# A two-layer hybrid decoder trunk: products that nothing reads on TensorE in the mixer, and the second attention group's score products over 128 rows

## The chip, the cores and the metric

The kernel runs on one core of a Trainium2 chip. TensorE (PE) multiplies matrices, VectorE (DVE), ScalarE (ACT) and GpSimd (POOL) do the rest, and SyncE (SP) issues most DMAs; POOL issues some too. The metric is the device time of one execution in microseconds; of several runs the median counts.

## The reference, cut to what matters

Two layers on x of 512 tokens by 1024 channels in float32. Each layer is a half-step SwiGLU feed-forward, a token mixer with three groups of heads, and a second half-step feed-forward; a layer norm follows each.

```
x = layer_norm(ALPHA * x + 0.5 * swiglu(x, ffn_a_gate, ffn_a_up, ffn_a_down))
aq, ak, av, bq, bk, bv, cc = split(x @ w_in)
o_a = rms_norm(diff_attention(rope(aq), rope(ak), av, lam)) * (1 - lambda_init)
o_b = rms_norm(dilated_attention(rope(bq), rope(bk), bv))
o_c, v_first = rwkv7_mixer(cc, ...)
x = layer_norm(ALPHA * x + concat([o_a, o_b, o_c]) @ w_out)
x = layer_norm(ALPHA * x + 0.5 * swiglu(x, ffn_b_gate, ffn_b_up, ffn_b_down))
```

Group A is differential attention, group B dilated attention (here one causal score matrix with a bias from the counts of its three patterns), group C RWKV-7 time mixing.

## The kernel before, in words

Every float32 operand of a large product is split into a high part, rounded to float32r, and a low part, the rest. A product is then three: high by high, high by low, low by high. The activations stand transposed, channels on partitions, in two tiles for the whole kernel, `xhi` and `xlo`, of 128 by 8 by 512 (channel within a block, block, token). A token block of 128 is written into them by `channel_ops`: for each half of the channels four PE transposes into a PSUM tile `m`, ACT's copy of it into `xhi`, DVE's difference into `xlo`. x0 to x3 are the four token blocks; x2 and x3 come late (`LATE`).

Accumulators in PSUM have the tags `p0`, `p1`, `m` and `r`, two buffers each. In a trace `p0` and `p1` both read p.

The two feed-forwards of a layer are long rows of products on PE. Between them stands the mixer, class `Mix`, whose engines follow an order written out by hand. Its parts are generators, named in `RANK` (line 1444), that yield the names of what they need next. `Board.merge` picks the next part whose needs are met at the time that the model gives PE, else the one whose needs are met first. The model is in `Board`: `free` is the time at which each engine is free, `ready` holds for each tensor the end of its last write, by tensor and not by the piece written, `slots` the times at which buffers of a tag came free. `Board.note` places each instruction: it starts when its engine is free and all tensors that it names are ready. `Watched` (line 470) records every mixer instruction there and then issues it, which is why they all bear line 504 in the profile. A DMA is taken to land 2 us after its transfer. The times exist only while the program is built; they set the order, and the hardware waits for semaphores.

In time a mixer goes: x2 and x3 arrive (`arrive`) while `columns` makes the input projection by 256-column products; group A's units, then group B's, run with the RWKV parts between them; then `out` forms the output product from the mixed heads, which `mixer_tiles` (tiles o) and `mixer_tiles_c` (tiles yc) transpose into `xhi` and `xlo`, blocks 0 to 5 and 6 to 7; then the norm, the transposes of the new x0 to x3, and `head`, the first products of the second feed-forward.

The attention groups read q and k from HBM, where `turner` wrote them; `fetch` loads them by POOL's DMA queue. For group B a unit of 128 queries makes its scores by two products: q high and low (128 rows, 64 each) by k high twice, and q high (64 rows) by k low, tile `k2`, 64 rows.

Of the kernel before, what the change touches and what calls it, by code (L numbers as in the profile page):

```python
# [9 lines left out]
FR = mybir.dt.float32r  # L10
# [6 lines left out]
S = 512  # L17
# [10 lines left out]
class Trunk:  # L28
    def __init__(self, ctx, tc, consts):
        self.tc, self.nc = tc, tc.nc  # L30
        pool = lambda name, **kw: ctx.enter_context(tc.tile_pool(name=name, bufs=1, **kw))
        self.const = pool("const")
        self.psum = pool("psum", space=PSUM)
        self.consts = consts
        self.xhi = self.const.tile([128, KD, S], FR, name="xhi")
        self.xlo = self.const.tile([128, KD, S], FR, name="xlo")
        self.open_x()
        kept = self.const.tile([128, 130], FT, name="kept")
        self.nc.sync.dma_start(kept, consts[:, 0:130])
        self.ident, self.pick = kept[:, 0:128], kept[:, 128:130]  # L40
        self.warmed = False
# [321 lines left out]
class Board:  # L363
# [6 lines left out]
    def __init__(self, tc):  # L370
        self.tc = tc
        self.free = {}
        self.ready = {}
        self.slots = {}
        self.events = {}
        self.last = self.late = 0.0
        nc = tc.nc
        for name, engine in (("pe", nc.tensor), ("vec", nc.vector), ("act", nc.scalar), ("pool", nc.gpsimd), ("sp", nc.sync)):
            self.free[name] = 0.0
            setattr(self, name, Watched(self, name, engine))  # L380
        self.free["dma"] = 0.0
# [18 lines left out]
    def note(self, name, fn, aps, cost):  # L400
        at = self.free[name]
        tiles = [self.ready.setdefault(a.tensor.name, [0.0, "", 0.0, None]) for a in aps]
        assert all(r[3] != "dropped" for r in tiles)
        dma = fn == "dma_start"
        for r in tiles[dma and tiles[0][1] == "dma":]:
            if r[1] != name or name != "pe":
                at = max(at, r[0] + 0.134)
        end = at + cost
        self.free[name] = end
        if dma:  # L410
            n = 4
            for d in aps[0].shape:
                n *= d
            end = max(end, self.free["dma"]) + n / 340e3
            self.free["dma"] = end
            end += 2.0
        for r in tiles:
            r[2] = max(r[2], end)
        tiles[0][0] = max(tiles[0][0], end)
        tiles[0][1] = "dma" if dma else name  # L420
        if dma:
            self.late = max(self.late, end)
        elif name != "pe":
            self.last = max(self.last, end)

    def when(self, spec, tail):
        at = 0.0
        need = {}
        for s in spec:
            if s == ".":  # L430
                at = max(at, tail)
            elif isinstance(s, str):
                if s in self.slots or s in TAGS:
                    need[s] = need.get(s, 0) + 1
                elif s in self.events:
                    at = max(at, self.events[s])
                else:
                    return None
            else:
                at = max(at, self.ready[s.tensor.name][0])  # L440
        for tag, n in need.items():
            free = self.slots.get(tag)
            if free is not None:
                if len(free) < n:
                    return None
                at = max(at, sorted(free)[n - 1])
        return at

    def merge(self, streams):

# [63 lines left out]
class Mix:  # L514


    def __init__(self, tr, pool, above, p, l, dram, v_first, small):
# [22 lines left out]
        self.kr, self.bk, self.am, self.bt, self.yt, self.uv, self.gam, self.key = {}, {}, {}, {}, {}, {}, [], []  # L540
        self.kd = dram.tile([2, 2, 128, S], FT, name=f"kr{l}")

    def run(self):
        with self.tr.tc.manual_schedule(engines=MANUAL):
            self.board.merge([getattr(self, name)(*args) for name, *args in RANK])
        return self.ahead

    def arrive(self):

        tr = self.tr  # L550
        for t in range(NT):
            self.board.ready[tr.x[t].tensor.name] = [ARRIVE[t], "vec", ARRIVE[t], None]
        self.board.free["vec"] = ARRIVE[-1]
        self.board.free["pe"] = START
        for t in LATE:
            yield from tr.channel_ops(t, self.pe, self.act, self.vec, self.acc, self.drop)
            self.mark(f"x{t}")
        for t in range(NT):
            self.sp.dma_start(self.spill[t], tr.x[t])
# [202 lines left out]
    def fetch(self):  # L762

        dma = self.gps.dma_start
        ap = lambda t, off, dims: bass.AP(tensor=t.tensor, offset=t.offset + off, ap=dims)
        for grp in "AB":
            for hp in range(3):
                for e in range(2):
                    yield f"qk{grp}{hp}", "x", "x"
                    if (hp, e) == (0, 0):  # L770
                        yield f"qk{grp}{hp}", "x", "x", "bias"
                        self.bias = self.get("bias", "bias")
                        dma(self.bias, self.tr.consts[:, 130:642] if grp == "A" else self.tr.consts[:, 642:1154])
                    a = self.get("x", "q", (128, 2, S), FR)
                    d = self.qk[grp, hp]
                    hi, lo, k = e * 64 * S, (256 + e * 64) * S, 128 * S
                    if grp == "A":
                        b = self.get("x", "k", (128, 2, S), FR)
                        dma(a[0:64], ap(d, hi, [[256 * S, 2], [2 * S, 32], [1, 2 * S]]))
                        dma(b[0:64], ap(d, hi + k, [[0, 2], [2 * S, 32], [1, 2 * S]]))  # L780
                        dma(a[64:96], ap(d, hi, [[2 * S, 32], [1, 2 * S]]))
                        dma(b[64:96], ap(d, lo + k, [[2 * S, 32], [1, 2 * S]]))
                    else:
                        b = self.get("x", "k2", (64, S), FR)
                        dma(a[:, 0, :], ap(d, hi, [[256 * S, 2], [S, 64], [1, S]]))
                        dma(a[:, 1, :], ap(d, hi + k, [[0, 2], [S, 64], [1, S]]))
                        dma(b, ap(d, lo + k, [[S, 64], [1, S]]))
                    self.qkt[grp, hp, e] = a, b
                    self.mark(f"q{grp}{hp}{e}")

# [428 lines left out]
    def attend(self, grp):  # L1219
        tr, vec, act, pe = self.tr, self.vec, self.act, self.pe  # L1220
# [5 lines left out]
        def scores(x):  # L1226
            hp, e, qt = x["id"]
            n = (qt + 1) * 128
            nn = max(n, 256)
            qs = slice(qt * 128, (qt + 1) * 128)  # L1230
            x["l"] = self.t("l", (128, 2), bufs=8)
            x["p"] = []
            a, b = x["qk"]
            for m in range(M):
                sc = self.acc("p1")
                if isA:
                    pe.matmul(sc[:, :nn], a[0:96, m, qs], b[0:96, m, :nn], start=True, stop=True)
                else:
                    pe.matmul(sc[:, :nn], a[:, 0, qs], a[:, 1, :nn], start=True, stop=False)
                    pe.matmul(sc[:, :nn], a[0:64, 0, qs], b[:, :nn], start=False, stop=True)  # L1240
                t = self.get("t", "t")
                nm = self.t("nm", (128, 1), bufs=8)
                vec.tensor_tensor_reduce(t[:, :n], sc[:, :n], bias[:, S - n:], scale, 3e38, op0=OP.add, op1=OP.min,
                                         accum_out=nm)
                self.drop(sc)
                act.activation(t[:, :n], t[:, :n], AF.Exp, scale=-1.0, bias=nm, accum_out=x["l"][:, m:m + 1])
                x["p"].append(t)
# [32 lines left out]
        units = [{"id": (hp, e, qt)} for hp in range(3) for e in range(2) for qt in range(NT)]  # L1280
        L1, L2, L3 = LAGS[grp]
        n = len(units)
        for i in range(n + L3):
            if i < n:
                x = units[i]
# [17 lines left out]
            if L1 <= i < n + L1:  # L1303
                x = units[i - L1]
                yield x["p"][-1], 
                combine(x)
            if L2 <= i < n + L2:
                x = units[i - L2]
                yield x["p"][0], "m", "aT"
                turn(x)  # L1310
            if L3 <= i < n + L3:
                x = units[i - L3]
# [127 lines left out]
                        yield ()  # L1440


LAGS = {"A": (1, 2, 3), "B": (1, 3, 4)}
RANK = [("arrive",), ("decays",), ("weights",), ("keys", 0), ("keys", 1), ("inside",), ("invert", 0), ("attend", "A"), ("scan",), ("attend", "B"), ("invert", 1), ("values",), ("turn_values",), ("fetch",), ("rwkv_out",), ("norms",), ("turner",), ("residual",), ("mixer_tiles",), ("columns",), ("out", 0), ("mixer_tiles_c",), ("out", 1), ("head",)]
MARGIN = 0.0
LATE = (2, 3)
START = 12.0
# [93 lines left out]
```

## Time and profile before

| | us |
|---|---|
| three runs | 2343.68, 2344.01, 2360.12 |
| median | 2344.01 |
| the profiled execution | 2363.04 |
| its span, first to last instruction | 2361.3 |
| PE busy in the span | 2250.8 (95%), 12384 products |
| VectorE, ScalarE, GpSimd busy | 1153.8, 804.7, 317.3 |
| mean granted clock of TensorE | 0.959 |

The page also cuts the span into 40 slices. In them PE is below 9 tenths only in the two mixers (slices 7 to 14 and 27 to 34, some 384 to 829 us and 1560 to 1994 us) and at the end, and the granted clock falls there too. TensorE's granted clock has two levels, 1.2 and 2.4 GHz; a granted share of 0.50 is the lower, 1.00 the higher, and a value between is a mean over a stretch. A matmul's end is modelled, so what a product costs is read from the distance between the starts of two that follow each other.

### The profile page before, as it was taken

What the parts mean: (1) busy time and instruction counts of PE and PEld (TensorE: products, weight loads), DVE (VectorE), ACT (ScalarE), POOL (GpSimd) and SP (SyncE); (2) the same over time, 40 slices, a digit from 0 to 9 for tenths busy, and PEclk for the clock granted to TensorE, in tenths of its full rate; (3) what the DMA queues carried; (4) which work ended last, traced back from release to release, by engine and by line L of the source; (5) the groups of instructions that cost most, each with busy time, mean ns of one, the idle gap of its engine ahead of it and who ended that gap; (6) DMA issues with size and microseconds to landing.
All of it is one profiled execution on the core that took longest, in us unless ns stands there. A gap on an engine that the chain in (4) does not pass through costs nothing.

```text
span 2361.3 us, 31781 instructions
## 1 busy us (share of the span) xinstructions
PE 2250.8 (95%) x12384; PEld 1878.7 (80%) x12384; DVE 1153.8 (49%) x2535; ACT 804.7 (34%) x1559; POOL 317.3 (13%) x344
## 2 busy tenths in 40 slices
PE   9999999987899999999999999999888998999998
PEld 8888888787777788888888888886877767888886
DVE  3333346666665633332653332567665667333336
ACT  4322233434444232222332222333454443222222
POOL 1000002343221300000010000023432222000000
PEclk9999999998887899999999999998998899999999
DMA  5333344354533223322543333443545333233334
GB/s 168 99 99 97 111 137 140 99 130 86 116 95 99 89 90 91 100 96 99 169 118 107 89 92 118 144 134 91 131 93 107 96 103 117 80 98 89 98 107 152
DMA packets 265702, 258.34 MB, mean 109 GB/s; under 512 B 56314, under 2 KB 213056, under 8 KB 265552
## 3 DMA queue, kind: packets, MB, share of 16 engines
q1 hardware_dynamic: 221488, 228.20, 32.0%
q0 software_dynamic: 43488, 27.06, 5.6%
q8 instruction: 97, 1.59, 0.3%
q10 hardware_dynamic: 576, 1.05, 0.1%
q14 instruction: 53, 0.43, 0.1%
HBM read 233.85 MB, written 22.28 MB: 108 GB/s over the span
## 4 chain that ended last, share of the span: by engine, by line
PE 81%; DVE 8%; DMA 5%; issue 3%; POOL 1%; ACT 1%; SPq 0%; POOLq 0%; DVEq 0%; ACTq 0%
PE p L86 18%; PE p L87 18%; PE p L85 18%; PE p L504 13%; PE r L504 4%; PE m L504 4%; DMA k<-qkA 3%; PE r L86 2%; PE r L85 2%; PE r L87 2%; DMA k<-qkB 1%; DVE x L504 1%; DVE rs_t L504 1%; POOL q L504 0%; POOL wl L504 0%
## 5 line engine op out<-in xcount | busy, mean ns | idle before, releaser
L80 DVE TENSOR_TENSOR lo<-raw,hi 128x1024 fp32r<-128x1024 f32 x300 | 366.2, 1223 | 634.9 <-ACT hi L79 634.3
L85 PE MATMUL p<-xhi,hi 128*128 128x512 f32 (+1 forms) x1392 | 538.0, 387 | 0.5 <-ACT xhi L118 0.5
L86 PE MATMUL p<-xlo,hi 128*128 128x512 f32 (+1 forms) x1392 | 537.7, 386 | 0.7 <-DVE xlo L119 0.7
L87 PE MATMUL p<-xhi,lo 128*128 128x512 f32 (+1 forms) x1392 | 537.5, 386 | 0.0
L79 ACT CAST hi<-raw 128x1024 fp32r<-128x1024 f32 x300 | 316.0, 1055 | 589.4 <-PE p L86 263.9
L86 PEld LDWEIGHTS p<-xlo,hi 128*128 128x128 f32 x1392 | 261.8, 188 | 58.8 <-DVE xlo L119 1.1
L85 PEld LDWEIGHTS p<-xhi,hi 128*128 128x128 f32 x1392 | 261.7, 188 | 58.8 <-ACT xhi L118 1.0
L87 PEld LDWEIGHTS p<-xhi,lo 128*128 128x128 f32 x1392 | 261.8, 188 | 57.9
L504 POOL TENSOR_TENSOR wl<-wr,wh 128x512 fp32r<-128x512 f32 x152 | 203.5, 1359 | 703.2 <-ACT wh L504 653.6
L504 PE MATMUL p<-wh,xhi 128*128 128x256 f32 (+1 forms) x704 | 236.1, 335 | 2.1 <-DVE rb L504 1.9
L504 PE MATMUL p<-wh,xlo 128*128 128x256 f32 (+1 forms) x704 | 219.9, 312 | 0.2 <-DVE xlo L504 0.2
L504 PE MATMUL p<-wl,xhi 128*128 128x256 f32 (+1 forms) x704 | 219.8, 312 | 0.0
L87 PE MATMUL p<-hi,hl 128*128 128x512 f32 x528 | 205.8, 390 | 0.0
L85 PE MATMUL p<-hi,hh 128*128 128x512 f32 x528 | 205.7, 390 | 0.0
L86 PE MATMUL p<-lo,hh 128*128 128x512 f32 x528 | 205.5, 389 | 0.0
L504 PEld LDWEIGHTS p<-wh,xhi 128*128 128x128 f32 x704 | 140.6, 200 | 13.3 <-PE p L504 2.3
L504 PEld LDWEIGHTS p<-wh,xlo 128*128 128x128 f32 x704 | 140.4, 199 | 7.0 <-DVE xlo L504 1.2
L239 DVE TENSOR_TENSOR hr<-p,hr 128x512 f32<-128x512 f32 x88 | 60.9, 692 | 172.8 <-PE p L87 163.3
L504 PEld LDWEIGHTS p<-wl,xhi 128*128 128x128 f32 x704 | 141.3, 201 | 4.3 <-POOL wl L504 0.3
L240 ACT CAST hh<-hr 128x512 fp32r<-128x512 f32 x88 | 54.3, 618 | 210.1 <-DVE hr L239 200.5
L504 ACT ACTIVATE t<-t,nm 128x128 f32<-128x128 f32 (+3 forms) x144 | 80.1, 557 | 128.0 <-DVE nm L504 127.0
L86 PEld LDWEIGHTS p<-lo,hh 128*128 128x128 f32 x528 | 99.1, 188 | 20.6
(247 smaller groups left out, 3104.3 us busy)
## 6 DMA issues: line engine op xcount, KB each, us to landing
raw<-in_ffn_a_down SPq DMA_DIRECT2D x66, 512.0 KB, 3.3
raw<-in_ffn_b_down SPq DMA_DIRECT2D x66, 512.0 KB, 3.4
raw<-in_ffn_a_gate SPq DMA_DIRECT2D x44, 512.0 KB, 3.8
raw<-in_ffn_a_up SPq DMA_DIRECT2D x44, 512.0 KB, 3.9
raw<-in_ffn_b_gate SPq DMA_DIRECT2D x40, 512.0 KB, 3.9
raw<-in_ffn_b_up SPq DMA_DIRECT2D x40, 512.0 KB, 3.8
wr<-in_w_in SPq DMA_DIRECT2D x56, 256.0 KB, 3.3
wr<-in_w_in SPq DMA_DIRECT2D x24, 512.0 KB, 3.8
```

Of the source, the lines that this page charges most:

```text
L79: nc.scalar.copy(hi, raw)
L80: (vec or nc.vector).tensor_tensor(lo, raw, hi.bitcast(FT), op=OP.subtract)
L85: mm(out, lh, rh, start=first, stop=False)
L86: mm(out, lh, rl, start=False, stop=False)
L87: mm(out, ll, rh, start=False, stop=last)
L239: nc.vector.tensor_tensor(hr, acc[1, f], hr, op=OP.mult)
L240: nc.scalar.copy(hi, hr)
L504: return call(*args, **kw)
```

## The change

The planner gets a further time, `worked`: until when PE has been busy by the model. When `note` places a PE instruction whose model start is later than that, `fill` puts in as many products as fit, `FILL` (0.1175 us) each, into a buffer of the tag whose free buffer has been free longest. Each is a 128 by 256 product of two pieces of `xhi`, block 7, tokens 384 to 511 as weights and 256 to 511 streamed. Nothing reads the result. They are issued past the recording layer, so that the planner does not know what they wait for. There are 404, 202 in each layer at the same places.

Apart from that, group B's tile `k2` holds k low twice over 128 rows, so that its load is 256 KB and not 128 KB, and the second score product takes all 128 rows of q.

```
+        if name == "pe":
+            self.fill(at)
+            at = max(at, self.free[name])
+            self.worked = at + cost
...
+    def fill(self, until):
+
+        n = int((until - self.worked) / FILL)
+        tags = {min(free): t for t in BANKS for free in [self.slots.get(t, [0.0])] if free and min(free) <= self.worked}
+        if n <= 0 or not tags:
+            return
+        ps = self.filler(tags[min(tags)], n)
+        self.worked += n * FILL
+        self.free["pe"] = max(self.free["pe"], self.worked)
+        self.ready[ps.tensor.name][2] = self.worked
+        self.drop(ps)
...
+    def filler(self, tag, n):
+        x = self.tr.xhi
+        ps = self.acc(tag, (128, 256))
+        for _ in range(n):
+            self.nc.tensor.matmul(ps, x[:, 7, 384:512], x[:, 7, 256:512], start=True, stop=True)
+        return ps
...
-                        b = self.get("x", "k2", (64, S), FR)
+                        b = self.get("x", "k2", (128, S), FR)
...
-                        dma(b, ap(d, lo + k, [[S, 64], [1, S]]))
+                        dma(b, ap(d, lo + k, [[0, 2], [S, 64], [1, S]]))
...
-                    pe.matmul(sc[:, :nn], a[0:64, 0, qs], b[:, :nn], start=False, stop=True)
+                    pe.matmul(sc[:, :nn], a[:, 0, qs], b[:, :nn], start=False, stop=True)
...
+BANKS = ("r", "m", "p0", "p1")
+FILL = 0.1175
```

Two places show how it stands on PE; all other PE instructions keep their order. The first is the start of layer 0's mixer: `m<-kept,x` are the transposes of x2 (x_65) and then x3 (x_66), and `p_2808` is an accumulator of the input projection over the tokens of x0 and x1. Before:

```order
L504 MATMUL m<-kept,x_65 128x128 x8
L504 MATMUL p_2808<-xhi,wh 128x256
L504 MATMUL p_2808<-xlo,wh 128x256
L504 MATMUL p_2808<-xhi,wl 128x256
L504 MATMUL m<-kept,x_66 128x128 x8
L504 MATMUL p_2808<-xhi,wh 128x256
L504 MATMUL p_2808<-xlo,wh 128x256
L504 MATMUL p_2808<-xhi,wl 128x256
```

And of the change, where the rows `<-xhi` with a count are the new products:

```order
L520 MATMUL m<-kept,x_65 128x128 x8
L563 MATMUL p_2835<-xhi 128x256 x7
L520 MATMUL p_2808<-xhi,wh 128x256
L563 MATMUL r<-xhi 128x256 x29
L520 MATMUL p_2808<-xlo,wh 128x256
L520 MATMUL p_2808<-xhi,wl 128x256
L520 MATMUL m<-kept,x_66 128x128 x8
L563 MATMUL r<-xhi 128x256 x7
L520 MATMUL p_2808<-xhi,wh 128x256
L563 MATMUL p_2903<-xhi 128x256 x6
L520 MATMUL p_2808<-xlo,wh 128x256
L520 MATMUL p_2808<-xhi,wl 128x256
```

Seven stand behind x2's transposes, 29 behind the first product after them, and 7 and 6 at the same places behind x3's.

The second is in the output product of layer 0: `m<-kept,yc` are the third pair of transposes of yc, `p_7024` and `p_7148` are the same accumulator of the output product, and `m<-uv,am` and `m<-st,kr` belong to the RWKV output. Before:

```order
L504 MATMUL m<-wa_1806,c 128x256
L504 MATMUL m<-kept,yc 128x128 x2
L504 MATMUL p_7024<-wh,xhi 128x512
L504 MATMUL p_7024<-wl,xhi 128x512
L504 MATMUL p_7024<-wh,xlo 128x512
L504 MATMUL m<-uv,am 64x64
L504 MATMUL m<-st,kr 64x64
```

And of the change:

```order
L520 MATMUL m<-wa_1806,c 128x256
L520 MATMUL m<-kept,yc 128x128 x2
L563 MATMUL r<-xhi 128x256 x4
L520 MATMUL p_7148<-wh,xhi 128x512
L520 MATMUL p_7148<-wl,xhi 128x512
L563 MATMUL r<-xhi 128x256 x9
L520 MATMUL p_7148<-wh,xlo 128x512
L520 MATMUL m<-uv,am 64x64
L520 MATMUL m<-st,kr 64x64
```

Four stand behind the transposes and nine behind the second product.

The orders of the other engines stay, but for one cast of feed-forward weights on ACT, and one difference of them on DVE, in each layer, which now stand ahead of x3's copies at the mixer's end.

## Rows read from the trace of the kernel before

Layer 0 is the first, layer 1 the second; the new products of layer 0's mixer would begin at 392.3 us of this trace, those of layer 1's at 1567.7.

**Rows 1.** Busy us by stretch: length, PE, PEld, DVE, ACT, POOL, granted clock, DMA, GB/s
```profile
392.32:708.52 316.20, 278.37 (x2243) 246.50 (x2242) 197.11 (x612) 136.60 (x396) 106.87 (x110) 0.90 0.42 105
708.52:829.27 120.75, 112.62 (x544) 89.73 (x544) 75.32 (x241) 39.76 (x118) 30.36 (x31) 0.80 0.30 92
1567.68:1889.65 321.97, 282.52 (x2251) 247.63 (x2249) 199.37 (x618) 141.02 (x401) 107.42 (x110) 0.89 0.42 103
1889.65:1994.23 104.58, 94.64 (x544) 74.27 (x544) 74.39 (x241) 39.42 (x118) 28.99 (x28) 1.00 0.35 104
```

**Rows 2.** PE in order of time, layer 1, start: start, us, instruction [idle before <-releaser]
```profile
1566.89 1.03 PE L504 MATMUL m<-kept,x 128*128 128x128 f32 x8
...
1567.68 0.36 PE L504 MATMUL p<-xhi,wh 128*128 128x256 f32 x1
...
1571.88 1.67 PE L504 MATMUL m<-kept,x 128*128 128x128 f32 x8 [3.60 <-DVE xlo L504]
...
1573.56 0.41 PE L504 MATMUL p<-xlo,wh 128*128 128x256 f32 x1
```

**Rows 3.** ScalarE's copies into xhi in order of time, layer 1
```profile
1567.52 1.07 ACT L504 CAST xhi<-m 128x512 fp32r<-128x512 f32 x2 [6.10 <-PE m L504]
...
1934.42 0.37 ACT L504 CAST xhi<-m 128x256 fp32r<-128x256 f32 x1 [5.70 <-PE m L504]
...
1993.94 1.18 ACT L504 CAST xhi<-m 128x512 fp32r<-128x512 f32 x2 [0.99 <-PE m L504]
```

**Rows 4.** PE in order of time, layer 0: spacing of 256-column products
```profile
384.46 0.28 PE L504 MATMUL p<-xhi,wh 128*128 128x256 f32 x1
...
391.41 0.28 PE L504 MATMUL p<-xhi,wl 128*128 128x256 f32 x1
...
398.50 0.41 PE L504 MATMUL p<-xlo,wh 128*128 128x256 f32 x1
...
401.49 0.41 PE L504 MATMUL p<-xhi,wh 128*128 128x256 f32 x1
```

**Rows 5.** Busy time by stretch, columns as in Rows 1
```profile
394.97:401.79 6.82, 5.26 (x25) 5.27 (x26) 3.48 (x6) 1.17 (x2) 0.00 (x0) 0.50 0.32 131
765.00:773.00 8.00, 8.00 (x36) 5.37 (x36) 1.60 (x7) 1.30 (x5) 1.26 (x1) 0.50 0.00 0
1572.56:1575.98 3.42, 3.42 (x17) 3.42 (x18) 1.38 (x2) 1.17 (x2) 0.00 (x0) 0.50 0.23 92
1922.00:1926.00 4.00, 4.00 (x27) 2.86 (x26) 1.77 (x8) 1.18 (x5) 0.00 (x0) 1.00 0.14 57
```

**Rows 6.** PE in order of time, layer 1, end of the second attention group
```profile
1912.60 0.66 PE L504 MATMUL m<-kept,t 128*128 128x128 f32 x4 [0.73 <-ACT aT L504]
...
1916.37 0.43 PE L504 MATMUL r<-v,aT 128*128 128x64 f32 x2 [0.47 <-ACT aT L504]
```

**Rows 7.** PE in order of time, layer 1, around the third yc transposes
```profile
1933.98 0.41 PE L504 MATMUL m<-kept,yc 128*128 128x128 f32 x2 [1.64 <-DVE yc L504]
...
1934.14 0.47 PE L504 MATMUL p<-wh,xhi 128*128 128x512 f32 x1
...
1935.45 0.33 PE L504 MATMUL m<-uv,am 128*64 128x64 f32 x2 [0.38 <-DVE gb L504]
```

**Rows 8.** PE in order of time, layer 1, transposes of x1 and x3
```profile
1980.22 1.25 PE L504 MATMUL m<-kept,x 128*128 128x128 f32 x8 [1.83 <-DVE xlo L504]
...
1993.25 1.25 PE L504 MATMUL m<-kept,x 128*128 128x128 f32 x8 [0.61 <-DVE xlo L504]
...
1994.25 0.37 PE L504 MATMUL p<-xhi,wh 128*128 128x256 f32 x1
```

**Rows 9.** Waits of PE (us in total, times, longest); DMA issues (KB, us to landing)
```profile
PE p L504 <- DMA k<-qkA: 41.4, 6, 10.8
...
q<-qkB POOLq DMA_DIRECT2D x24, 256.0 KB, 10.0
...
k<-qkB POOLq DMA_DIRECT2D x12, 128.0 KB, 9.8
```

More of the change, by code (lines that the diff above doesn't have):

```diff
@@ L375, in __init__ @@
         self.events = {}
-        self.last = self.late = 0.0
+        self.last = self.late = self.worked = 0.0
         nc = tc.nc
@@ L541, in __init__ @@
         self.kd = dram.tile([2, 2, 128, S], FT, name=f"kr{l}")
+    def filler(self, tag, n):
[4 more added lines that the diff above has]
+        return ps
     def run(self):
+        self.board.filler = self.filler
         with self.tr.tc.manual_schedule(engines=MANUAL):
@@ L553, in arrive @@
         self.board.free["vec"] = ARRIVE[-1]
-        self.board.free["pe"] = START
+        self.board.free["pe"] = self.board.worked = START
         for t in LATE:
```

## The prediction

> **What bounds the kernel now.** I read the granted clock by stretch first, then TensorE's (PE's) order of time around the places where the change puts its products, then the waits. The four stretches [rows 1] are, for each layer, the mixer from its first new product to the end of the second attention group, and its tail (end of that attention, output product, norm, first gate and up products). PE is busy 278.4 of 316.2 us, 112.6 of 120.8, 282.5 of 322.0 and 94.6 of 104.6. So PE is the bound almost throughout, and what is added to it is paid unless an idle stretch follows that something else ends. The granted clock is 0.90, 0.80, 0.89 and 1.00. As it has two levels, 1.2 and 2.4 GHz, a mean of 0.90 over 316.2 us is 63 us at the lower one; the four give 63, 48, 71 and 0 us. The two tails hold the same 544 products, and the one with 48 us at 1.2 GHz is 16.2 us longer (120.75 against 104.58). That is the prize: what a tail at full clock is worth.
>
> It is a prize only where it is lost. The profiled execution took 2363.0 us (span 2361.3). The runs took 2343.7, 2344.0 and 2360.1. 2363.0 less the 16.2 of layer 0's tail is 2346.8, within 3 us of the two fast ones; so I take the median, 2344.0, for an execution in which both tails run at full clock as layer 1's did here, and there the tail has nothing to give.
>
> **The price of one product.** The same form (128 rows, 256 columns, new weights each) starts 60 times between 384.46 and 391.41: 6.95 us over 59 steps, 0.118 us each at full clock [rows 4]. At half clock 15 of them from 398.50 to 401.49 give 0.214. 404 are 47.5 us, or 86 if all met the low clock; no row excludes either end. I take 0.118, since most stand where the clock of layer 1 is 1.00.
>
> **Where they stand.** The real products keep their order on PE; 202 are added in each layer. In the trace PE has no idle time at nearly all of those places: the next product starts at once. The planner notes readiness for a whole tensor; a copy that writes one token block of xhi makes it expect a wait of products that read other blocks. So a new product is cover only for idle time that comes a few instructions later. A second price: the new products read xhi[:, 7, 256:512], the last two token blocks. Behind the transposes of a block that writes this piece they wait for ScalarE's copy, and all later products wait with them; before, PE went on with another block.
>
> The sum per layer, at full clock, with layer 1's rows:
> - Start, 49 products. Before: transposes of x2 at 1566.89, next product 1567.68, then 3.60 us idle until x3 at 1571.88 [rows 2]. The copies of x2 end at 1568.59 (1567.52 + 1.07) [rows 3]: 0.91 of waiting. Then 7 products (to 1569.4), one real, 29 (to 1572.9), two real: x3's transposes start at about 1573.2, 1.3 late. They take 0.8, their copy again some 0.9, 13 products 1.5 and a real one 0.1: 1576.5, where before the second product stood at 1573.56 [rows 2], 2.95 late. Filling the wait keeps the clock up: before, 1572.56 to 1575.98 ran at 0.50 [rows 5], 2.4 us of it behind 1573.56, where at full clock 1.1 is saved. Net 1.9. In layer 0 the low spell is longer (394.97 to 401.79 [rows 5]) and 0.5 more comes back: 1.4.
> - Three single ones in the middle: 0.35.
> - End of the second attention, 51: 6.0 us, less the idle times of 0.73 and 0.47 at 1912.60 and 1916.37 [rows 6], at which eleven and one of them stand: 4.8.
> - After the sixth group's transposes, 17: 2.0 us, against 1.64 idle that VectorE's yc ends at 1933.98 [rows 7]: 0.4.
> - After the third yc transposes, 4 and 9: the copy ends at 1934.79 (1934.42 + 0.37) where PE went on at 1934.14, so 0.65, and 1.5 for the products, less 0.38 of idle at 1935.45 [rows 3, 7]: 1.8.
> - 14 before the second half's products: 1.6. Four after the last yc: 0.65 + 0.5 = 1.15. No idle time follows that they don't shift as well.
> - After x0, 12: 1.4 against 1.83 idle until 1980.22 [rows 8], which VectorE ends: 0. After x1, 11: 1.3.
> - After x2, 15: 0.9 for the copy and 1.8, less 0.61 idle [rows 8]: 2.1. After x3, 13: the copies end at 1995.12 against a product at 1994.25 [rows 3, 8]: 0.9 + 1.5 = 2.4.
>
> That is 17.8 and 17.3: 35 us in all. Behind it PE goes straight on in the next feed-forward, which is PE-bound, so nothing hides it. A product also takes a PSUM slot and so waits for the slot's last reader; the planner takes the slot that has been free longest, so I take 0. If each of the 14 runs at the attention's end found its slot still being read, at the 0.65 of a copy it would be 9 us a layer, 18 in all; that bounds the range above.
>
> **The wider score product.** Its columns are the same, so PE pays nothing. Its load grows from 128 to 256 KB, six times a layer, on POOL's queue. 128 KB lands in 9.8 us and 256 KB in 10.0 in that queue [rows 9]: 0.2 us, and the new products ahead of it delay the need by more: 0. If size cost its share, twelve loads of which the later ones come just in time would cost 2 us. Of the clock it changes little: PE kept the full clock from 1922 to 1926 with 64-row and 64-column products, and the half clock from 765 to 773 with the same ones [rows 5]; so the level goes by what went before, an idle stretch in most cases, not by the rows of the array in use. The largest idle stretches, six waits of together 41.4 us for k<-qkA [rows 9], get no product, because the planner expects those loads early.
>
> **A rule against the change.** PE shows no idle at the places, and a product that waits holds its successors [rows 2, 7]. The Trainium skill ("TensorE: Matmul & The Clock Gate", section "Step-by-step: what each phase is for") says that only weight loads are pulled ahead and products stay in program order; by that the copy's wait is paid in full, as in the sum. The same page's section "HAM oscillation — how this bites in real kernels" speaks for the change: idle gaps re-throttle the clock, and the loss is half of the throttled time. By that the four stretches lose 91 us (half of 182); the trace's own tails show 16.2 for 48, a third.
>
> **The sum.** 2344.0 + 35 = 2379, 1.5% more. From the profiled execution: 2363.0 - 16.2 (layer 0's tail at full clock, since the eleven products of [rows 6] stand at the same idle time there) + 35 = 2382, the same within the 3 us between that execution and the runs. I take 2379.
>
> **Rivals.**
> - Low tails in the median too. If one of the two tails still had its 48 us in the 2344 us runs, the new products return 16.2: 2363. For it: the clock fell in one layer and not in the other at equal work. Against: the distance from 2344 to 2360 is one such tail.
> - Not slower: the middles hold the full clock. Shifted waits and wider scores would have to lift the clock between 408 and 708 and between 1576 and 1890: 134 us at half clock less 10 at the starts, less the 41 us waited for loads, is 83 us of work, half of which is 41: 2338. It decides from 70 us of these 83 on. Against: no new product stands in those waits, so I see no mechanism that reaches most of it.
> - The planner is right: the products fall into idle time and cost nothing, the two starts return 2: 2342. Against: PE's rows at the places.
> - Worse: one tail still falls to half clock in the median run, though the products stand in it: 16 for the spell and about 99 of them at 0.214, 9 more: 2404. It decides when the waits for the copies, which are idle time themselves, bring the clock down.
>
> **How the numbers follow.** Forecast 0.62 (own range 2368 to 2397: without the waits for copies, some 11 us in both layers, below; with the 18 us for PSUM above), low tails 0.15, middles 0.10, planner right 0.05, worse 0.08. From 2350 to 2398 lie the forecast and the low tails, about 0.8 with what of the worse case comes out smaller. About 1% (23 us) is what a measurement of this kernel can tell from no change. Slower by over 1% (above 2367.4): 0.60 of the forecast and the worse case, 0.68. Faster (below 2320.6) needs middles and tails together: 0.04. Within 1%: 0.28.
>
> **What would show it.** In the changed profile: 404 products of 128x256 from xhi, 0.118 apart; idle time behind x2's and x3's transposes ended by ACT's xhi, 0.6 to 0.9 us each; the 3.60 us wait at the starts gone and the clock there 1.0; both tails at clock 1.0 and about 104.6 + 14 to 16 us long; the k<-qkA waits still near 41 us. The forecast is wrong if a tail is shorter than 113 us, or if the middles' clock is above 0.95.

## The result, and the profile after

| | before | after |
|---|---|---|
| median of the runs, us | 2345.9 (2343.2 to 2360.8) | 2367.0 (2364.7 to 2376.3) |
| ratio to before, 95% interval | 1 | 1.0085 (1.0059 to 1.0111) |
| the profiled execution | 2363.0, span 2361.3 | 2370.6, span 2368.8 |
| mean granted clock | 0.959 | 0.971 |

The change costs 20 to 21 us, 0.85% by the ratio. I had forecast 35 us, 1.5%. The direction was right, and so was the price of the products. But the time is 12 us under the forecast and 1 us below the forecast's own range, 2368 to 2397; only the wider range, 2350 to 2398, which takes in the low tails, held. The ratio lies within the 1% to which I had given 0.28. Two terms that I had put at nothing make the difference, as shown below. The profiled execution of after is 3.7 us longer than its median. One execution of the kernel before, of 7463 us, is left out of all ratios.

The busy time of after by stretch, between the same products of PE as in [rows 1] (columns as there: length, PE, PEld, DVE, ACT, POOL, granted clock, DMA, GB/s):

```profile
394.51:705.84 311.33, 274.32 (x2287) 245.61 (x2285) 195.82 (x602) 134.53 (x394) 107.69 (x110) 0.91 0.44 105
705.84:825.34 119.50, 109.69 (x688) 94.48 (x687) 79.37 (x247) 43.15 (x122) 30.74 (x31) 0.97 0.34 99
1566.40:1882.32 315.92, 279.44 (x2295) 249.13 (x2294) 197.27 (x609) 139.03 (x399) 108.25 (x110) 0.91 0.43 104
1882.32:2000.67 118.35, 109.96 (x689) 95.02 (x687) 79.30 (x247) 42.90 (x122) 29.16 (x28) 0.97 0.33 97
```

Both tails (lines 2 and 4) now have the same clock, 0.97, and nearly the same length. Against the tail that ran at full clock before, 104.58 us in [rows 1], they are 14 to 15 us longer; against the one at 0.80, 120.75 us, the first is 1.3 us shorter. The clock of the two long stretches before them, 0.91, is hardly better than the 0.90 and 0.89 of before: outside the starts only three new products a layer stand there.

PE in order of time at the start of layer 1's mixer, which answers to [rows 2] (start, us, instruction, idle before and its releaser):

```profile
1565.46 1.10 PE L563 MATMUL p<-xhi 128*128 128x256 f32 x7 [0.73 <-ACT xhi L520]
1566.40 0.28 PE L520 MATMUL p<-xhi,wh 128*128 128x256 f32 x1
1566.52 3.64 PE L563 MATMUL r<-xhi 128*128 128x256 f32 x29
1569.99 0.28 PE L520 MATMUL p<-xlo,wh 128*128 128x256 f32 x1
1570.11 0.28 PE L520 MATMUL p<-xhi,wl 128*128 128x256 f32 x1
1570.23 1.03 PE L520 MATMUL m<-kept,x 128*128 128x128 f32 x8
1571.99 1.09 PE L563 MATMUL r<-xhi 128*128 128x256 f32 x7 [0.73 <-ACT xhi L520]
```

The 3.60 us of idle time are gone, 29 products at 0.12 us stand in them, and behind each group of transposes PE waits 0.73 us for ScalarE's copy, because the new products read what it writes. Over the whole program PE's waits (us in total, times, longest) are, for [rows 9]:

```profile
PE p L520 <- DMA k<-qkA: 42.9, 6, 10.4
PE p L520 <- DMA k<-qkB: 6.7, 6, 1.7
PE r L563 <- ACT xhi L520: 6.2, 10, 0.7
PE p L563 <- ACT xhi L520: 1.5, 2, 0.7
```

The six long waits for k<-qkA stand as they stood, 42.9 against 41.4 us. New are twelve waits for ScalarE, 7.7 us, and the waits for k<-qkB, which were 0.4 us in two places.

### The profile page after: what moved, and what is told of

Same layout as the page of the kernel before. It is cut to its first block, busy times and chain, and to the rows that moved or that the text cites. A ratio compares the mean times of both kernels' runs of the same rounds, so it can differ in the third digit from the quotient of the medians.

```text
span 2368.8 us, 32591 instructions
## 1 busy us (share of the span) xinstructions
PE 2260.4 (95%) x12788; PEld 1908.6 (81%) x12788; DVE 1157.7 (49%) x2535; ACT 803.7 (34%) x1559; POOL 319.5 (13%) x344
## 4 chain that ended last, share of the span: by engine, by line
PE 85%; DVE 6%; DMA 5%; issue 2%; ACT 1%; POOL 1%; SPq 0%; DVEq 0%; POOLq 0%; ACTq 0%
PE p L86 18%; PE p L87 18%; PE p L85 18%; PE p L520 14%; PE r L520 4%; PE m L520 4%; DMA k<-qkA 4%; PE r L87 2%; PE r L86 2%; PE r L85 2%; PE r L563 1%; DMA k<-qkB 1%; DVE x L520 1%; DVE rs_t L520 1%; PE p L563 0%
## 5 line engine op out<-in xcount | busy, mean ns | idle before, releaser
L520 PE MATMUL p<-wh,xhi 128*128 128x256 f32 (+1 forms) x704 | 228.4, 324 | 1.2 <-DVE rb L520 1.2
```

Source lines behind the costliest of these rows:

```text
L520: return call(*args, **kw)
```

## The experiments

The first four experiments, the next four and the last three were each measured on another chip, beside the kernel before (medians 2343.6, 2341.7 and 2339.4 us). So kernels are compared by their ratios to it, and a difference of two ratios is uncertain by some 0.003, 7 us.

**The kernel before, again.** No edit.

> The kernel before, unchanged, profiled a second time. Theory A (the 3 us difference between the profiled execution without its low tail and the fast runs is small change, and the middles of the mixers are as in the first profile): about 2345 us, and the two middles, from the first new product's place to the end of the second attention group, take 316 and 322 us again, with 55 to 65 us each at half clock. Theory B (the middles differ from execution to execution by several us, and this is where the sum of 35 and the measured 21 part): the middles move by more than 4 us, with another set of half-clock spells, and so does the total.

Measured: 2343.3 us, ratio 1.0001 (0.9978 to 1.0024). Its profiled execution took 2344.1 us, the median that I had argued about without a profile of it. Its four stretches, cut as in [rows 1]:

```profile
393.83:704.30 310.47, 274.99 (x2242) 243.32 (x2240) 198.70 (x612) 136.34 (x396) 106.86 (x110) 0.91 0.43 107
704.30:808.94 104.64, 94.51 (x545) 74.28 (x544) 74.39 (x241) 39.44 (x118) 30.79 (x31) 1.00 0.35 106
1546.94:1861.79 314.85, 280.10 (x2250) 245.24 (x2249) 199.52 (x619) 140.91 (x401) 107.45 (x110) 0.90 0.41 104
1861.79:1975.23 113.44, 105.89 (x545) 84.70 (x544) 74.92 (x241) 39.69 (x118) 28.95 (x28) 0.86 0.32 96
```

The tail of layer 1 (line 4) ran at 0.86, that is 32 us at half clock, and is 8.8 us longer than that of layer 0. So an execution of 2344 us need not have both tails at full clock, as I had taken. The two long stretches are 5.7 and 7.1 us shorter than in [rows 1], so theory B's sign came: they differ by more than 4 us between two executions of one kernel. Of the 19.0 us between the two spans, 2361.3 and 2342.3, 12.9 lie in the long stretches and 7.3 in the tails; the rest went the other way by 1.2.

**Only the wider score product and its larger load**, no new products.

```
-                        b = self.get("x", "k2", (64, S), FR)
+                        b = self.get("x", "k2", (128, S), FR)
...
-                        dma(b, ap(d, lo + k, [[S, 64], [1, S]]))
+                        dma(b, ap(d, lo + k, [[0, 2], [S, 64], [1, S]]))
...
-                    pe.matmul(sc[:, :nn], a[0:64, 0, qs], b[:, :nn], start=False, stop=True)
+                    pe.matmul(sc[:, :nn], a[:, 0, qs], b[:, :nn], start=False, stop=True)
```

> The kernel before with only the second part of the change: group B's second score product over 128 rows and its load of 256 KB; no product is added. Theory A, as in the prediction (rows of the array don't matter to the clock, and the load is covered): ratio 1.000, within 0.002, and the half-clock spells between 600 and 720 us as before. Theory B (the wider products raise the clock in group B's part, which is where the changed kernel's middles got 4 and 6 us shorter): about 2335 us, ratio 0.995 to 0.997, with fewer us at half clock in 600 to 720 and 1780 to 1900.

Measured: 2338.7 us, ratio 0.9985 (0.9966 to 1.0005): theory A's number, at most a small gain and no loss. The rows of PE show why it can be a gain at all. A unit of group B in the kernel before, layer 1, with 384 columns:

```profile
1894.82 0.42 PE L504 MATMUL p<-q 128*128 128x384 f32 x1
1895.17 0.44 PE L504 MATMUL p<-k,q 64*128 64x384 f32 x1
1895.55 0.50 PE L504 MATMUL p<-wh,xhi 128*128 128x512 f32 x1
```

The same unit in after:

```profile
1889.13 0.43 PE L520 MATMUL p<-q 128*128 128x384 f32 x1
1889.39 0.34 PE L520 MATMUL p<-k,q 128*128 128x384 f32 x1
1889.57 0.40 PE L520 MATMUL p<-wh,xhi 128*128 128x512 f32 x1
```

From start to start the two score products took 0.35 and 0.38 us with 64 rows in the second, and 0.26 and 0.18 with 128. The columns are the same; the product of 64 rows delays both itself and its successor, 0.29 us a unit here. There are 24 units a layer; those of 256 and of 512 columns show 0.28 and 0.29 us, wherever PE runs at full clock and waits for no load.

**Only the new products**, score products and k2 as before.

> The kernel before with the 404 products only; group B's scores stay at 64 rows. Theory A (the products alone make the difference): 2367 us, ratio 1.0085, as the whole change. Theory B (the wider scores gave 10 us back in the middles): 2377 us, ratio about 1.013.

Measured: 2377.2 us, ratio 1.0144 (1.0116 to 1.0172), theory B's time. The 404 products cost 34 us (27 to 40).

**The whole change, but the products read a small tile that is written once.** They then wait for no copy.

```
+        self.still = self.const.tile([128, 8], FR, name="still")
+        self.nc.vector.tensor_copy(self.still, self.ident[:, 0:8])
...
-        x = self.tr.xhi
+        x = self.tr.still
...
-            self.nc.tensor.matmul(ps, x[:, 7, 384:512], x[:, 7, 256:512], start=True, stop=True)
+        w, y = (x[:, 0:1].to_broadcast([128, k]) for k in (128, 256))
+            self.nc.tensor.matmul(ps, w, y, start=True, stop=True)
```

> The whole change, but the 404 products read a small tile that is written once at the start, so that they never wait for a copy into xhi. Theory A (the sum: five waits for copies of 0.65 to 0.9 us in each layer, 8 to 10 us in all): 2367 less 8 to 10, about 2358, ratio to before 1.005. Theory B (the waits cost nothing, since the products behind them would have waited too): 2367 as the whole change.

Measured: 2360.2 us, ratio 1.0074 (1.0048 to 1.01). The whole change stands at 1.0085, and at 1.0106 in the repetition below. So this kernel gains some 3 to 7 us, less than the 11 that I had put on the copies' waits; the intervals overlap, and the size is no better known than that. Nor is all of it the waits: here the new products also stand closer together. The 29 of layer 1's start take 3.24 us from the first to the next real product, 0.112 each, where after has 3.47 us, 0.120 each:

```profile
1562.94 3.41 PE L566 MATMUL r<-still 128*128 128x256 f32 x29
1566.18 0.28 PE L522 MATMUL p<-xlo,wh 128*128 128x256 f32 x1
```

For 404 products that is some 3 us. What is left, 17 us, is the products' own time less what the wider score product and the clock return.

**The wider score product without the larger load.** k2's upper 64 rows are set to zero, which leaves the scores as they are, and the load stays at 128 KB.

```
-                        dma(b, ap(d, lo + k, [[0, 2], [S, 64], [1, S]]))
+                        dma(b[0:64], ap(d, lo + k, [[S, 64], [1, S]]))
+                        self.nc.gpsimd.memset(b[64:128].bitcast(FT), 0.0)
```

> The kernel before with the wider score product alone, but tile k2's upper 64 rows are set to zero by GpSimd and its load stays at 128 KB, so that the scores are the same numbers. It parts the two halves of the wider product: the shorter spacing of score products on PE, and the load that is twice as large. Theory: PE takes about 0.28 us less for each of 24 units a layer, 13 us in all at full clock, and the larger load eats the most of it (waits for k<-qkB of 0.9 us before, 3.0 us in the wider product alone, 6.7 us in the whole change). Then this kernel stands 6 to 13 us under the kernel before (ratio 0.995 to 0.9975), below the wider product alone (0.9985), and its waits for k<-qkB are under 1.5 us. Rival: the load costs nothing and the shorter spacing is absorbed by other waits (softmax on VectorE and ScalarE); then the ratio is that of the wider product alone, 0.998 to 1.000, and PE waits longer for aT or t instead.

Measured: 2328.8 us, ratio 0.9953 (0.9937 to 0.9969), 11 us under the kernel before. The theory's time came: the shorter spacing gains about 11 us, and the kernel with the load that is twice as large stands some 7 us behind it (2 to 13, by ratios from two chips). But its sign in the waits did not come:

```profile
PE p L504 <- DMA q<-qkB: 4.8, 4, 1.9
PE p L504 <- DMA k<-qkB: 2.3, 6, 0.9
```

The waits for k<-qkB are shorter than in the whole change, but not under 1.5 us, and PE now waits for q<-qkB. Together they are 7.1 us, where the kernel with the larger load had 4.3 (3.0 and 1.3). So the 7 us are not in these waits. In the two profiled executions they are in the tails, with the larger load and then here:

```profile
701.32:808.35 107.03, 94.45 (x544) 75.63 (x543) 74.17 (x243) 39.39 (x118) 31.06 (x31) 0.97 0.34 106
1858.57:1970.66 112.09, 100.48 (x544) 80.78 (x543) 74.32 (x243) 39.49 (x118) 29.14 (x28) 0.89 0.33 99
```

```profile
695.43:799.64 104.21, 92.01 (x545) 73.57 (x543) 74.30 (x243) 39.54 (x118) 32.02 (x33) 1.00 0.34 107
1855.93:1959.99 104.06, 91.77 (x543) 73.46 (x542) 74.19 (x243) 39.50 (x118) 30.20 (x30) 1.00 0.34 104
```

The tails differ by 10.9 us and by their granted clock, the long stretches by less than 1 us (620.8 and 621.5 together). Over all executions the mean granted clock gives 150 us at half clock with the larger load and 130 here. Whether the load brings the clock down, and by what, no run shows.

**Products in the waits for k<-qkA alone**, with the wider score product: 20, 68 and 43 in each layer, placed by a table and not by the planner.

```
+        if name == "pe":
+            self.fill(GAPS.get((self.layer, self.count), 0))
+            self.count += 1
...
+GAPS = {(0, 732): 20, (1, 736): 20, (0, 958): 68, (1, 962): 68, (0, 1234): 43, (1, 1238): 43}
```

> The kernel before with the wider score product (0.9985 alone) and 131 products that nothing reads in each layer, all in the three waits of group A's first unit of each head pair for k<-qkA (20, 68 and 43 products: 2.4, 8.0 and 5.1 us at 0.1175 each, under the shortest waits that the traces show there, 2.4, 8.3 and 5.1). None stands where the change puts its own. Theory: the clock falls because PE idles there, 57 us at half clock follow these six waits in the wider product's trace, and what PE loses in them sets when buffers come free for the next load; the products hold the clock, about half of the 57 us comes back, 20 to 28 us: ratio 0.986 to 0.991, with under 20 us at half clock behind these waits. Rival 1: the next wait, for a load or for ScalarE, ends when it did and takes it all up: ratio 0.997 to 1.000, waits for k<-qkA and others longer by as much. Rival 2: what is left of the waits is still enough for the clock to fall: the half-clock spells stay, ratio 0.998 to 1.000.

Measured: 2328.7 us, ratio 0.9944 (0.9921 to 0.9966): 10 us under the wider product alone (by ratios from two chips, so uncertain by 7), half of the least that was expected. The longest of the waits, in the kernel with the wider product alone and then here:

```profile
545.02 0.28 PE L504 MATMUL p<-wh,xlo 128*128 128x256 f32 x1
554.45 0.77 PE L504 MATMUL p<-k,q 96*128 96x256 f32 x2 [9.15 <-DMA k<-qkA]
...
556.93 0.41 PE L504 MATMUL p<-wh,xlo 128*128 128x256 f32 x1
557.14 0.41 PE L504 MATMUL p<-wh,xhi 128*128 128x256 f32 x1
```

```profile
545.00 8.33 PE L556 MATMUL p<-xhi 128*128 128x256 f32 x68
553.16 0.61 PE L513 MATMUL p<-k,q 96*128 96x256 f32 x2
...
554.62 0.28 PE L513 MATMUL p<-wh,xlo 128*128 128x256 f32 x1
554.74 0.28 PE L513 MATMUL p<-wh,xhi 128*128 128x256 f32 x1
```

Without products the 256-column products behind the wait start 0.21 us apart, with them 0.12. The stretch of group A's units in both layers, from its first score product on, without and with:

```profile
514.77:639.39 124.62, 103.51 (x1014) 97.41 (x1014) 82.35 (x286) 62.50 (x212) 41.98 (x47) 0.88 0.47 102
1673.69:1796.66 122.97, 103.03 (x1014) 96.67 (x1014) 82.64 (x286) 62.33 (x212) 41.98 (x47) 0.90 0.46 103
```

```profile
516.20:630.62 114.42, 108.58 (x1125) 102.27 (x1125) 82.97 (x286) 62.24 (x212) 42.00 (x47) 1.00 0.48 110
1673.74:1791.97 118.23, 111.55 (x1125) 105.16 (x1125) 82.25 (x286) 62.20 (x212) 41.99 (x47) 0.97 0.46 106
```

The clock rises from 0.88 and 0.90 to 1.00 and 0.97, and 10.2 and 4.7 us come back. The us at half clock are twice what the clock lacks: 30 less in the first stretch and 17 less in the second, so that one of them is worth a third to a quarter of a us, not half. Some 7 us at half clock are left, so the forecast's sign (under 20) came, and neither rival did. That PE waits for what other engines and loads bring in these stretches would explain the rest; no run parts that.

**Products in ten further idle times**, by the same table: 131 more in each layer, 524 in all.

> As the kernel with products in the waits for k<-qkA, and 131 more in each layer in ten other idle times that every trace without products shows at the same places, each filled to 70 to 85 per cent: before x3's transposes at the start (26 products in 3.6 us), before the second attention inputs' and RWKV transposes (8, 16, 8, 20 and 16), before the third yc transposes (12), before the transposes of x0 and x1 in the tail (13, 6 and 6). Theory: products that end before the wait does cost PE nothing and hold the clock; some 70 us at half clock behind these places are left by the other kernel, and a third to a half of what they lose comes back, another 10 to 18 us: ratio 0.978 to 0.987. Rival 1: they make PE late where the wait is shorter than in the traces, or make copies into xhi wait, as the change's own products do; then this kernel is slower than the one with products in the waits for k<-qkA alone, by 3 to 10 us. Rival 2: what the clock gives back in these stretches ends in waits for VectorE, ScalarE or loads: the same within 4 us.

Measured: 2312.0 us, ratio 0.9876 (0.986 to 0.9892), 17 us under the run before it, in the expected step; the ratio itself is just outside the expected 0.978 to 0.987, as the run before it stood higher than was put. The 524 products are 62 us of PE at 0.118 each, and the time falls all the same, since they stand where PE was idle. The span and mean clock:

```profile
core 0: 2306.0 us, clock 0.990
```

With the wider product alone the profiled execution had 0.968 over 2337.7 us, 150 us at half clock; here it is 46. These 104 us gave back 26 (0.9985 less 0.9876 of 2343), again a quarter.

**The whole change with half of the products**, 182.

```
-FILL = 0.1175
+FILL = 0.235
```

> The whole change with FILL at 0.235 us, so that each place gets about half of its products: 182 and not 404, in the same order with everything else. Theory A, a product costs its own time wherever it stands: half of the 34 us that the products alone cost, so 17 us less 10 for the wider score product: ratio 1.002 to 1.004. Theory B, only what runs over the end of the real wait costs: the start's 21 products of 2.5 us fit in its 3.6 us and cost nothing, the tails' lie more often within their waits, so that less than half of the price is left, 6 to 12 us: ratio 0.997 to 1.001. Theory C, the tails' clock falls again with half of the products: 30 to 50 us at half clock in a tail, and the ratio is 1.003 to 1.010 with tails no shorter than 119 us.

Measured: 2349.3 us, ratio 1.0036 (1.0016 to 1.0055), theory A's number. Theory C's range holds it too, but not its tails, which were to be no shorter than 119 us. At the start theory B holds: there 14 products stand in the wait and x3's transposes still wait 0.54 us behind them:

```profile
394.26 1.84 PE L563 MATMUL r<-xhi 128*128 128x256 f32 x14
396.87 1.25 PE L520 MATMUL m<-kept,x 128*128 128x128 f32 x8 [0.54 <-DVE xlo L520]
```

From the start of x2's transposes to the fourteenth real product behind x3's it takes 9.2 us, where the kernel before run again has 9.6. So the price is paid in the tails: the first is 111.05 us long at 0.97 by the cut of [rows 1], where the whole change has 119.50 and a tail without products, at full clock, 104.64. Over all executions this kernel has 140 us at half clock, as many as the kernel before beside it, so half of the products returned nothing by the clock.

**The whole change again, and without the products of the tails.** The first has no edit. In the second the planner counts the time of the products behind group B's last score, but none is issued.

> The whole change again, beside the next two kernels on one chip, so that they can be set against it there: 1.0085 was measured, 1.006 to 1.011 expected. Theory of its price: the products alone cost 34 us, of which the tails hold two thirds, and the wider score product gives back 10.

```
+        self.worked += n * FILL
+        if "attended" in self.events:
+            self.free["pe"] = max(self.free["pe"], self.worked)
+            return
         ps = self.filler(tags[min(tags)], n)
-        self.worked += n * FILL
```

> The whole change without the products that the planner puts in after group B's last score product: 90 products are left in each layer (49 at the start, 3 single ones, 38 between the score products of group B's end), and 112 are gone from each tail; the planner still counts their time, so that all else stands in the same order. My working put 12 us a layer on those 112 (1.2 for a quarter of the end of attention B, then .4, 1.8, 1.6, 1.15, 0, 1.3, 2.1, 2.4). Theory: a tail costs what its products and the copies behind them cost, and its clock is no worse without them than in the kernel before; then 24 us go and the ratio is 0.996 to 1.000. Rival: the products did pay in the tails by holding the clock (7 us at half clock in each tail of the whole change, up to 48 without products); then a tail without them is 110 to 116 us long with 20 to 48 us at half clock, not 106, only 8 to 14 us go, and the ratio is 1.002 to 1.005.

Measured: 2364.6 us, ratio 1.0106 (1.0085 to 1.0127), for the whole change, and 2349.3 us, 1.0043 (1.0022 to 1.0064), without the tails' products. The trace has 92 products a layer, not 90; 110 are gone. They cost 15 us (8 to 22) and not 24; the rival's time came, with fewer us at half clock than it put. The tails without them:

```profile
703.62:813.10 109.48, 100.02 (x584) 83.16 (x583) 75.30 (x243) 40.06 (x118) 30.87 (x31) 0.94 0.35 104
1867.12:1977.87 110.75, 101.32 (x584) 83.75 (x583) 75.35 (x243) 40.05 (x118) 29.37 (x28) 0.92 0.33 101
```

They are 10.0 and 7.6 us shorter than in after, but at 0.94 and 0.92, where after has 0.97 twice. One execution would not show this, since tails without products differ by more; but over all executions the mean granted clock gives 140 us at half clock here (nine executions) and 124 in the whole change beside it (four). So the products did hold the clock, and took more for it than it was worth.

**The measured idle times and the zeroed k2 together.**

> The kernel with products in the measured idle times (26 places, 0.9876), and k2's upper rows set to zero by GpSimd instead of loaded twice (0.9953 against 0.9985 for the score product alone). Theory: the two are separate gains, the load's 3 to 7 us come on top, since in the former kernel PE still waited 5.7 us for group B's loads and a half-clock spell of 7 us followed the longest: ratio 0.983 to 0.986, 2303 to 2311 us if the kernel before stands at 2343. Rival: with the clock held the load is no longer what PE waits for longest in group B (softmax is), and nothing comes on top: 0.987 to 0.989.

Measured: 2306.8 us, ratio 0.9864 (0.9838 to 0.9889). Against 0.9876 this is no difference that can be told; the interval holds both theories' numbers, so whether the smaller load still brings something with the clock held stays open. It is the shortest median of all kernels here, 33 us under the kernel before. It and the former table's kernel beat both the kernel before and the change by the same idea, with the products where PE is idle.

## Why the prediction was right or wrong

**The starts: right.** The 3.60 us wait is gone and the clock is full there. From the start of x2's transposes to that of the fourteenth real product behind x3's it takes 11.5 us in each layer of after, and 9.6 and 9.1 in the kernel before run again: 1.9 and 2.3 us more, where I had 1.4 and 1.9.

**The tails' own price: right.** By the cut of [rows 1], which ends at the first real product behind x3's transposes, my terms are 14.9 us a layer (4.8, 0.4, 1.8, 1.6, 1.15, 0, 1.3, 2.1, and 0.9 with seven products behind x3's). Against tails at full clock, 104.64 us in the kernel before run again and 104.58 in [rows 1], those of after are 14.9 and 13.8 longer, with 0.03 of the clock missing, about 7 us at half clock each, so that some 2 us of the 14.9 and 13.8 are the clock's. I had put the clock there at 1.0. The waits for the copies are 0.73 us, as put (0.65 to 0.91).

**That both tails of the median run at full clock: wrong, the step that failed.** I read it from one difference, 2363.0 less 16.2. Most of that difference lay elsewhere: 12.9 of 19.0 us in the long stretches, as the kernel before run again shows. The 2344.1 us execution had one tail at 113.44 us. Against it the new products return 8.8 us, which my sum did not give them. "Low tails in the median too", a rival to which I gave 0.15 and 16 us, was half true. The spans of after and of the kernel before run again differ by 26.5 us: 14.9 in the first tail, 4.9 in the second, 1.9 in the two long stretches, and 4.8 in what lies ahead of, between and behind these four.

Those are two executions. The span and the mean granted clock are on record for every one. The 68 of the kernel before beside the experiments have 142 us at half clock in the mean (117 to 179), the 12 of the whole change 127. A straight line through the 68 rises by 0.32 us for each us at half clock (correlation 0.86). So what the clock returns is some 5 us in the mean, and not 8.8 or 0; the mean clock does not tell in which stretch.

**The wider score product, 0: wrong, the other mis-sized term.** "Its columns are the same, so PE pays nothing" looked at the product and not at its neighbours. PE takes about 0.3 us less for a unit, 11 us in all when the load does not grow, and 4 us with the larger load (0.9985); in the profiled executions the 7 us between them lie in the tails and their granted clock, and how the load would bring that about stays open. Beside the new products it seems worth more, 1.0144 less 1.0085 or 1.0106, 9 to 14 us, but the uncertainty of these is 8 to 9 us. The profiled executions help no further: from group A's first score product to group B's first, the products alone had 34 and 33 us at half clock and the kernel before run again 25 and 30, but its first execution had 33 and 33.

The Trainium skill ("TensorEngine Tiling (Array Packing)", section "Key Properties") says that a change of the tiling mode drains TensorE; in the section "Available Configurations" there the Trainium skill lists modes of 128, 64 and 32 rows. The 64-row rows above agree with it: the 64-row product and the one behind it start late. That a drain is the cause no run shows. The 96-row products of group A, for which the Trainium skill lists no mode, are not late; in the kernel with products in all idle times

```profile
514.68 0.28 PE L513 MATMUL p<-wh,xlo 128*128 128x256 f32 x1
514.80 0.63 PE L513 MATMUL p<-k,q 96*128 96x512 f32 x2
515.27 0.38 PE L513 MATMUL m<-kept,t 128*128 128x128 f32 x2
```

two of them with 512 columns take 0.47 us, four times the 0.118 of 256 columns, and the product ahead keeps its 0.12. I had not weighed this rule, and it speaks for the change.

**The sum of 35 for the products alone: 34 measured, within 7.** The kernel with the products alone has 131 us at half clock in the mean, 15 less than the kernel before on the same chip (146), at 0.32 some 5 us; so my sum should have been 30, which the interval holds. With these 5 us and the 4 to 14 us of the wider score product taken off, 35 becomes 16 to 26; the whole change measured 20 and 25.

**The rule of half the throttled time.** The prediction set the half of the Trainium skill ("TensorE: Matmul & The Clock Gate", section "HAM oscillation — how this bites in real kernels"), 91 of 182 us, against the third of the trace's tails and did not use it. The runs bear the trace out: a third to a quarter, and 0.32 over the 68 executions.

**The waits for k<-qkA: right.** They got no products and stayed, and it is there that products pay. The first test of the forecast, a tail under 113 us, and the second, a clock of the middles above 0.95, both stayed away, as they should.

## What to carry to other kernels

Work that only keeps the clock up paid here where the trace shows the engine idle, and cost its own time elsewhere: take the places and the lengths from the trace, not from the planner's model, and let the products read what is long written. The kernels that gained left a part of most waits unfilled; whether that is needed was not tried. Before such work is priced, look at the span and the granted clock of many executions, since the one that was profiled may be another case, even when its time is the median. And look at what stands behind a product of fewer rows: it pays too.

## What the hardware showed that I had not expected

- A product of 64 rows between products of 128 starts 0.09 us later and delays the next by 0.20 (0.35 and 0.38 against 0.26 and 0.18 us); one of 96 rows shows no such price.
- A us at half clock is worth a third to a quarter of a us in this kernel, where PE is busy 95% of the span: 10.2 us for 30, 26 us for 104, and 0.32 us each over 68 executions of the kernel before.
- Two tails of equal work, at half clock for 48, 32 or 0 us in different executions of the same kernel; the time of an execution does not tell which (2363 and 2344 us each had one low tail).
